# A chunked delta-rule recurrence on TensorE: products of a head pair on 64x128 and 128x128 stationaries, v and y turned on the whole array, and a new order of instructions

## The chip, the cores and the metric

The kernel runs on one core of a Trainium2 chip. The metric is the device time of one execution in microseconds, lower is better. Five engines work beside each other, each in its own program order: TensorE (PE, with its weight loads listed apart as PEld), VectorE (DVE), ScalarE (ACT), GpSimd (POOL) and SyncE (SP, which issues the DMAs here).

## The reference

Two layers over 256 positions of width 2048, batch 1. Layer 0 is an RWKV-7 time mix, a recurrence over time with a 64x64 state for each of 32 heads, then a squared-ReLU MLP. Layer 1 is forgetting attention over shared keys and values, then another MLP. The change lies in the recurrence and what surrounds it:

```python
def rwkv7_recurrence(r, decay, k, v, a, b):
    # S_t = S_{t-1} diag(decay_t) + (S_{t-1} a_t) b_t^T + v_t k_t^T ;  y_t = S_t r_t
    ...
y = rwkv7_recurrence(rh, dh, kh, vh, -kk, kk * ah)
mu = jnp.mean(y, axis=-1, keepdims=True)
var = jnp.mean(jnp.square(y - mu), axis=-1, keepdims=True)
y = ((y - mu) * lax.rsqrt(var + LNX_EPS)).reshape(B, S, D)
y = y * lnx_w + lnx_b
bonus = jnp.sum(rh * kh * r_k, axis=-1, keepdims=True) * vh
out = ((y + bonus.reshape(B, S, D)) * g) @ w_o
```

## The kernel before

Activations lie transposed: 128 channels on the partitions, 256 positions along the free axis, 16 such tiles (`xT`, and the operands `opA`, `opB`, each split into a high and a low part). A large product reads its weights in pieces of 512 KB (`load_split`): SP issues the load of `wr`, ACT casts it to the high part `wh`, DVE subtracts to the low part `wl`, and TensorE multiplies high by high, high by low and low by high, in fp32r, 12 products per step of 128 input rows (`mm3`, `gemm_steps`). The small products of the recurrence are plain fp32, and the profile lists each of these as two instructions.

The 32 heads are worked in eight units `u` of four heads. A tile of 128 partitions holds two heads, h = 0 on the lower 64 partitions (`HA`) and h = 1 on the upper (`HB`); q = 0, 1 are the two tiles of the unit. Time is cut into four chunks c of 64 positions. For each unit

- `prep` makes decays, keys and the scaled vectors and stores them to scratch in HBM;
- `inv` builds a 64x64 triangular inverse for each head and chunk, by fp16 products on 64x64 quarters of the array;
- `rec` (`rec_steps`) does the recurrence. It loads r, k, b, v and the inverse; forms the masked products of the keys and b with r (`g2a`, `g2b`) and with a diagonal of decays (`bta`, `btb`), 32 products 64x64x64 in each of two steps, on all four quarters of the array; the bonus sums (`bs`, 16 products with one column); then four chunks of three dependent steps. In the first, z from the state (`zp`, a 128x64 stationary); in the second, u = inverse times z (`up`, 64x64) and r times the state (`yp`, 64x64); in the third, the new state (`sp`) and y (`yp`), both on 128x64 stationaries from `L2`. Between the steps DVE and ACT copy the result out of the bank `zyus` (`zt`, `Tt`, `yt`). At the end come the group norm of y, 32 products 64x64 that turn y back (`yp`) and multiply v by the bonus (`vp`), the gain `lnw`, the bias `lnb`, the gate, and the split into `opA`.

The order of the work is written out by hand for each engine. Each generator is a stream (`gk`, `gr`, `gv` and `wo` are the large products, `la`, `lw`, `lg` and `gate` the low-rank ones, `mk`, `mr`, `mv` their inputs). `record` cuts each stream into pieces by step and engine; `ORDER_A` and `ORDER_B` list these pieces, as `rec3P` for the next TensorE piece of unit 3, and `replay` issues them in that order. Stage A covers projections and part of the inverses; stage B, the recurrence and the rest, with `gv` and `wo` pieces in between. After the replay the rest of the `wo` product (k = 12 to 15), the MLP and layer 1 follow, which the change leaves alone but for the order of the rows of `w_o`.

Of the kernel before, what the change touches and what calls it, by code (L numbers as in the profile page):

```python
# [94 lines left out]
STREAMS_A = (["first", "h", "mk"] + [f"gk{g}" for g in G4] + ["la", "lw", "lg", "gate"] + [f"prep{u}" for u in range(8)]  # L95
# [3 lines left out]
firstG firstP lwQ*2 gk0Q firstS gk0Q prep0Q*2 firstP firstV*2 firstS firstP firstG firstV firstP firstV firstP  # L99
firstS*2 hV*2 hG hV*2 hG lwV hV hG lwP lwV hV hG lwP gk0S lwV hG hV gk0S lwP lwV hG hV lwP lwV gk0S hG lwV lwP gk0S  # L100
mkV hG lwP gk0V mkS lwV*2 lwP mkV gk0V lwP gk0P mkV gk0Q hV gk0Q mkS gk0V hG mkV*2 gk0P lwV mkS gk0V mkV laQ mkV lwP
laV gk0P mkS hV gk0S mkV hG gk0S mkV gk0P gk0V mkS lwV gk0S mkV gk0S gk0V lwP gk0P mkV gk0Q gk0V mkS mkV*2 laP gk0V
gk0P mkS mkV gk0Q mkV laV mkS gk0P laV mkV hV gk0S mkV laP hG gk0S hV gk0P laV mkS hG gk0V mkV laP gk0S gk0V laP gk0S
lwV gk0P laQ lwV mkV gk0V mkS lwP mkV lwP gk0V gk0P mkV gk0Q laV mkS laV laP mkV hV laP mkV gk0P hG laV mkS laV mkV hV
laP lwV laP hG mkV gk0P gk0S gk0Q laV mkS gk0V gk0S mkV lwP gk0V laP lwV gk0P gk2Q mkV laV mkS hV lwP mkV hG hV laP
gk0S laV gk0P hG lwV gk0S mkV gk0V mkS lwP mkV laP gk2S gk0V gk0P gk2S lwV gr3Q mkV laV mkS lwP gk2V laP lwS mkV gr3Q
lwS gk2P mrV lwS laV mrS lwV laV mrV laP gk2V laP gr3S gk0P mrV gk2Q laV gr3S laV mrS gr3V laP gk0S mrV laP prep0S mrV
gk2P gr3Q prep0S gk0V prep0S gr3V prep0S gr3P lgV gr3Q laS prep0V mrS gr3S mrV gr3S mrV prep0P gr3V gk2S prep0P prep0V
mrS gk2S gr3P mrV prep0S mrV prep0S gr3V prep0S gr3P gk2V gk2Q prep0S gk2V mrS gr3S lgV gk2P gr3Q mrV gr3S gr3V mrV
gr3P gr3V gr3S mrS gr3V gr3Q gr3P mrV gr3S mrV gr3V mrS gk2P mrV gk2Q gk2S mrV gk2V mrS gr3P mrV gk2S mrV gk2V mrS  # L110
prep0P mrV gr3S gr3Q mrV gr3P gr3V mrS prep0S mrV prep0S mrV prep0S gk2P mrS prep0S mrV gr3S mrV gr3P gr3S gr3V mrS
gr3V prep0S gr3Q gr3P mrV gr3S mrV prep0S gr3V mrS gk2P gk2S prep0V gk2Q mrV gk2V gr3P gk2S mrV prep0V mrS mrV gr3P
gr3S gk2V mrV gk2Q gr3V mrS gk2P gr3S mrV prep0V mrV gr3P prep0S gr3V mrS prep0Q gr3S prep0V gk1Q mrV prep0S gr3P
prep0S prep0V gr3V gr3S lgV gr3V gr3P gk2S prep0V gk1Q gk2V prep0Q gk2P gk2S prep0V*2 gk2V prep0Q gr3P prep0V gk2S
gk1Q prep0V gk2V prep1S prep0Q gr3P prep1S prep0V gk2S prep0Q gk2V gk2P gr3S gr3V gk1S gr3Q prep1S gr3Q gk1V gk2P gk1Q
prep1S inv0Q gk1S prep1V gk2P gk1V gk1S gk1V gk1Q inv0Q prep1P gk1S prep1P inv0Q prep1V gk1V gk1P prep1S prep2Q prep1S
gk1Q prep1S gk1P prep1S gk1S gk1V gk1P gk1S gk1V gk2P gk1Q gk1S gk1V gk1P gk1S gk1V prep1P gk1Q gk1S gk1V gk1P prep1S
prep2Q prep1S*2 gk1P prep1S gk1S prep1S gk1V gk1P gk1S lgQ prep1S gk1V gk1P prep1V gk1S prep1V gk1V gk1P gk1S prep1V
gk2Q gk1V prep1S gk1P prep1V gk1S prep1Q prep1V*2 prep1S*2 gk1V gk1P prep1Q gk1S prep1V*2 gr0Q gk1V prep1Q gk1P gk1S
prep1V gk1V gk1P prep1V gk2S gr0Q prep1V prep1Q gk2V gk1P prep1Q gk2S gk2V gk1P lgQ gr0S gr0V gk1P gr0S gr0V lgP gr0Q  # L120
gk1S gk1V prep2S gk2P lgV prep2S*3 lgP gr0S prep2V gr0S gr0P gr0V*2 lgV prep2P gr0Q prep2P prep2V gr0S prep2P prep2S
gr0V prep2S lgP prep2S*2 gr0P lgV prep2S*3 lgP prep2S*2 gr0P lgV lgQ prep2S gr0S prep2V lgP gr0S prep2V gr0P prep2V*2
prep2S prep2V*2 prep2S*2 gk2P prep2Q prep2V*2 prep2Q gr0S prep2V prep2Q lgP prep2V*2 gr0P prep3S prep2Q prep3S gr0V
prep2Q gr0V gr0Q lgP gr0V gr0P lgV gk2Q lgV prep3S lgV prep3S gr0P prep3V prep3P*2 prep3V prep3P prep3S prep4Q prep3S
lgP prep3S prep4Q prep3S gr0P lgV gr0Q prep3S*3 lgP prep3S gr0S lgP lgV gr0S gr0V lgP gk2S gr0V gk2S gr0P gk2V lgQ
prep3S gk2V gr0S lgV prep3S gk2P gr0Q gr0V gr0S lgV gr0V gr0P prep3V gr0Q prep3V gr0P prep3V*2 prep3S prep3V*2 prep3S
lgP prep3S prep3Q prep3V*2 prep3Q gr0S gr0P gk3Q lgV gr0S prep3Q gr0V*2 lgP gr0S prep3V gk3Q gr0S gr0P gr0V*2 lgV lgP
gk3Q prep3V gr0P prep3V prep3Q mvV gk3S prep3Q lgP gk3V gk3S gk3V gk2P gk3Q gr0P gk3S gk2V gk2S gk3V prep5S lgP
prep5S*2 gr0P gr2Q prep5S lgS prep5V lgS gk3P gr0V lgS gr0S prep5P gk3S gr0Q prep5P mvS gr0Q prep5V gk3S mvV prep5P
gk3S gk3V prep5S gk3P gk3V prep5S gr2Q prep5S gk3V prep5S mvV gr2Q gk3P prep5S*3 gk3P prep5S*3 gk3P mvS prep5V gk3S  # L130
prep5V gk3S gk3P prep5V gr2S*2 mvV gk3V prep5S inv0P gk3V gr2S prep5Q inv0P prep5S gr2V prep5S gr2Q gk3P inv3Q inv0V
inv3Q inv0V inv0S inv3Q gr2V inv0Q gr2P gr2S inv0V gr2Q gr2V*2 gr2P gr2S mvV gk3Q gr2V mvS gk3P mvV gr2S mvV prep5V
mvS gr2V gr2P gr2S mvV gr2Q mvV gr2V mvS gr2P mvV gr2S mvV gr2V mvS inv3P mvV gr2Q mvV inv3P prep5V mvS prep5V inv0P
gr2S inv2Q gr2P inv3V inv2Q*2 inv3V inv3S prep5Q inv0V inv3Q gr2P gr2S inv3V inv0V*2 inv3P gk3S gr2V inv0P inv3V gr2P
inv3V*2 inv3P inv0V gk3S gr2P inv3V gr2V gk3V inv3P gr2Q gr2S inv0P gk3V inv3S gr2P gr2V gateQ inv3S mvV inv0S mvV
inv0S inv3P prep5V*2 gr2S inv2P inv3V inv2P mvS prep5Q gr2V inv0P inv1Q gk3P inv2V inv1Q*2 inv2V inv2S gk3Q inv0V
inv3P inv2Q gr2S mvV gr2P inv3S mvV inv3S gr2V mvS prep5V inv3P gr2S mvV inv0P inv3V inv0S gr2P gr2V inv0S mvV gk3Q
inv3P prep5V gr2S inv0P prep5V inv3S prep5Q gr2P inv3S inv0V prep5Q prep4S gr2V prep4S inv3P prep4S inv0P inv3V prep4S
gr2P inv0S prep4V inv0S gr2S inv3P inv0P gk3S gr2V prep4P inv3S inv0V gr2P gk3Q inv3S prep4V gk3V inv3P gk3S inv0P
inv3V inv0S prep4P gk3V inv0S inv3P prep4S gv0Q prep4S inv0P prep6Q inv3S inv0V gr2P inv3S prep4S inv3P prep4S gk3S  # L140
inv0P inv3V inv0S prep4P inv2V gk3V inv0S inv3P prep4S prep6Q inv2P prep4S inv3V inv0P prep4S inv2V gr2P inv3Q prep4S
inv2V prep4S inv2V prep4S inv0V gk3P gr2S prep4V gk3S gr2Q prep4V gateP gk3S prep4V mvS prep4V prep4S prep4V*2
prep4S*2 gk3P prep4Q prep4V*2 prep4Q gateS prep4V prep4Q gk3P gateQ prep4V gk3S prep4V prep4Q gr2V gk3P prep4Q gv0S
gk3V gr2Q gk3V gv0Q gk3P gv0S gk3V gv0V gv0Q gk3P gv0V mvV gv0Q mvV gk3P mvS mvV*2 mvS gateP gk3V gk3S prep6S mvV
prep6S mvV prep6S inv2P gateV gv0Q prep6S inv0P inv1P inv2V gv0S gateQ inv1P gv0S inv0V gv0P inv0Q mvS inv1V gv0S
inv4Q gv0V inv4Q inv1S gv0P gv0V inv4Q gv0S inv1V gateQ prep6V inv1Q gv0P gv0S gv0V*2 inv2P gv0S gv0V gr1Q gv0P inv2S
gv0V inv2S inv1V gv0Q mvV prep6P gv0S mvV gv0P prep6V mvS gv0V gv0P mvV gv0S mvV gv0V mvS gv0P mvV gr1Q mvV mvS inv4P
mvV inv4P inv2P inv4V inv5Q inv1P inv5Q gateP inv4V inv4S inv5Q inv2V inv4Q inv1V gr1S gateP inv1V gateS gr1V gr1S
gateQ inv1V gv0P gr1V gr1Q gateV gv0Q gateQ prep6P gv0S gv0V gv0P prep6S*3 gr1P prep6S gv0S gv0V gv0P gr1S gateQ gr1V
gr1P gr1S gr1V gv0P gr1Q gr1S gr1V gr1P gr1S gr1V gr1P gv0Q gv0S gv0V prep6P gv0S gv0V gv0P prep6S*2 gr1Q prep6S gr1P  # L150
prep6S gr1S prep6S gr1V gv0P gr1S prep6S gr1V gr1P gv0S prep6V gr1Q gv0V gr1P prep6V gv0S prep6V gv0V prep6S gv0P
prep6V gr1S gr1Q prep6V*2 prep6Q prep6S*2 gr1P gr1V gr1S prep6Q prep6V*2 gr1V gv0P prep6Q gr1S prep6V gr1Q gr1V gr1P
gr1S prep6V gr1V prep7S prep6Q gv0P prep7S prep6V gv1Q gr1S prep6Q gr1V gr1P gv0S gv0V prep7S gv0Q prep7S gv0Q gateP
gv0Q gr1S prep7V gv0Q*2 gr1V gr1S gv0Q prep7P gr1V gv0Q prep7P gv0Q prep7V gv1Q prep7P prep7S*2 gateP prep7S*4 gr1P
gv1Q prep7S gateV prep7S*2 inv2P inv1P prep7S inv1V gr1P gateS prep7V inv2S gateQ inv2S prep7V gateQ gr1P gr1S prep7V
# [99 lines left out]
def trunk_kernel(ctx: ExitStack, tc: tile.TileContext, xin, vecs, bfv, c32, c16, w_rkv, w1, w2, a1, a2, g1, g2,  # L255
# [360 lines left out]
    pp = ppctx.enter_context(tc.tile_pool(name="proj", bufs=1, reuse_waits="tile"))  # L616
    hT = pp.tile([P, KT, T + 1], F32, name="hT")
    dT = xT
    gh = pp.tile([P, 2, T], F32, name="gh")
    rs = gh[:, 0, :]  # L620

    def first_steps():
# [730 lines left out]
```

## Time and profile before

| | us |
|---|---|
| median of 3 runs (lowest, highest) | 2446.46 (2446.16, 2447.48) |
| the profiled execution's own time | 2446.65 |
| its span, first to last instruction | 2444.9 |
| PE busy in the span | 2407.0 |
| DVE, ACT, POOL busy | 1520.3, 1246.9, 217.0 |
| first and last product of `zyus` start | 343.9, 569.3 |

A busy time counts an instruction from its start to its modelled end; products overlap, so that the busy time of a group of products is not their price. The price of one is read from the distance between starts. A product's row gives the stationary as rows*columns and then the moving operand. An idle time is given with what ended it; "issue" there means that nothing the profile shows was waited for.

### The profile page before, as it was taken

Reading aid. Unit: us, or ns where it says so; the run is one execution under the profiler, and the core shown is the slowest. Engines: PE = TensorE matmul, PEld = TensorE weight load, DVE = VectorE, ACT = ScalarE, POOL = GpSimd, SP = SyncE. Lnnn points to the kernel's source line nnn. Section 1 sums busy time; section 2 is a strip of 40 time slices with the busy share of each in tenths; the row PEclk is TensorE's granted clock in tenths of the full one; section 3 lists DMA queues with packets and bytes.
Section 4 is the critical chain, followed back from the end, with each engine's and each line's share of the span. In section 5 each row is a group of like instructions: output and inputs, shape, how many; then the busy total and the mean of one; then the engine's idle time right before and its main releaser. Section 6 shows DMA issues by size and latency. Waiting matters only on the chain.

```text
span 2444.9 us, 45691 instructions
## 1 busy us (share of the span) xinstructions
PE 2407.0 (98%) x18336; PEld 2077.2 (85%) x18336; DVE 1520.3 (62%) x2210; ACT 1246.9 (51%) x1983; POOL 217.0 (9%) x218
## 2 busy tenths in 40 slices
PE   8999999999999999999999999999999999999998
PEld 6999877789888888888888888888888888888886
DVE  8878767766754555555567555877654555555554
ACT  3767655545544543443545545555554543443543
POOL 2000012221200000000101000101100000000101
PEclk9999999999999999999999999999999999999999
DMA  5766786656656656666655566545656666666653
GB/s 166 238 230 233 258 262 192 185 184 204 206 190 192 192 187 195 190 189 197 187 185 172 179 193 192 169 150 186 201 184 196 189 190 192 192 187 196 189 188 122
DMA packets 276564, 472.55 MB, mean 193 GB/s; under 512 B 23280, under 2 KB 70656, under 8 KB 276352
## 3 DMA queue, kind: packets, MB, share of 16 engines
q1 hardware_dynamic: 276352, 469.64, 61.3%
q8 instruction: 143, 2.34, 0.4%
q14 instruction: 69, 0.57, 0.1%
HBM read 445.44 MB, written 24.13 MB: 192 GB/s over the span
## 4 chain that ended last, share of the span: by engine, by line
PE 92%; DVE 4%; issue 2%; DMA 1%; ACT 0%; POOL 0%; SPq 0%; POOLq 0%; DVEq 0%; ACTq 0%
PE mmw L245 32%; PE mmd L245 28%; PE mm L251 9%; PE mmn L245 7%; PE mmv L251 4%; PE mmv L245 4%; PE zyus L251 2%; PE i L251 1%; DVE wl L251 1%; PE lps L251 1%; PE mm L245 1%; DVE xs L251 1%; PE lo L251 1%; PE mmg L251 1%; DVE wl L245 0%
## 5 line engine op out<-in xcount | busy, mean ns | idle before, releaser
L245 DVE TENSOR_TENSOR wl<-wr,wh 128x1024 fp32r<-128x1024 f32 (+1 forms) x784 | 810.0, 1044 | 698.4 <-ACT wh L245 623.1
L245 ACT CAST wh<-wr 128x1024 fp32r<-128x1024 f32 (+1 forms) x784 | 702.6, 901 | 833.2 <-PE mmd L245 344.3
L245 PE MATMUL mmw<-opB,wh 128*128 128x512 f32 x1280 | 321.2, 393 | 0.2 <-ACT wh L245 0.2
L245 PE MATMUL mmd<-wh,opA 128*128 128x512 f32 x1024 | 315.8, 390 | 0.0
L245 PE MATMUL mmd<-wh,opB 128*128 128x512 f32 x1024 | 315.8, 390 | 0.0
L245 PEld LDWEIGHTS mmw<-opB,wh 128*128 128x128 f32 x1280 | 230.3, 189 | 42.2 <-ACT wh L245 0.4
L245 PE MATMUL mmw<-opA,wh 128*128 128x512 f32 x1024 | 256.7, 392 | 0.0
L245 PEld LDWEIGHTS mmd<-wh,opA 128*128 128x128 f32 x1024 | 191.7, 188 | 39.5
L245 PEld LDWEIGHTS mmd<-wh,opB 128*128 128x128 f32 x1024 | 191.7, 188 | 39.5
L245 PEld LDWEIGHTS mmw<-opA,wh 128*128 128x128 f32 x1024 | 184.4, 189 | 33.3 <-ACT nln L245 0.3
L251 ACT CAST wh<-wr 128x512 fp32r<-128x512 f32 x240 | 144.9, 617 | 116.4 <-PE mm L251 50.1
L245 PE MATMUL mmd<-wl,opA 128*128 128x512 f32 x512 | 199.3, 389 | 0.0
L245 PE MATMUL mmd<-wl,opB 128*128 128x512 f32 x512 | 199.2, 389 | 0.0
L251 DVE TENSOR_TENSOR wl<-wr,wh 128x512 fp32r<-128x512 f32 x240 | 169.3, 719 | 38.3 <-ACT wh L251 32.1
L245 PEld LDWEIGHTS mmw<-opB,wl 128*128 128x128 f32 x1280 | 174.5, 190 | 13.5 <-DVE wl L245 1.0
L245 POOL TENSOR_TENSOR ms<-mt 128x512 f32<-128x512 f32 x64 | 78.5, 1239 | 1158.8 <-ACT mt L245 1158.8
L245 PE MATMUL mmw<-opB,wl 128*128 128x256 f32 x1280 | 178.6, 282 | 0.6 <-DVE wl L245 0.6
L251 PE MATMUL mm<-opA,wh 128*128 128x256 f32 x896 | 171.4, 291 | 0.2 <-DVE opA L251 0.2
L245 PEld LDWEIGHTS mmw<-opA,wl 128*128 128x128 f32 x1024 | 139.7, 190 | 10.0
L251 PEld LDWEIGHTS mm<-opA,wh 128*128 128x128 f32 x896 | 141.7, 192 | 3.8 <-DVE opA L251 0.4
L245 PE MATMUL mmw<-opA,wl 128*128 128x256 f32 x1024 | 142.8, 282 | 0.0
L251 PE MATMUL mm<-opA,wl 128*128 128x256 f32 x448 | 127.2, 284 | 0.0
(273 smaller groups left out, 3338.0 us busy)
## 6 DMA issues: line engine op xcount, KB each, us to landing
wr<-in_mlp_w_up_dram SPq DMA_DIRECT2D x256, 512.0 KB, 4.1
wr<-in_mlp_w_down_dram SPq DMA_DIRECT2D x256, 512.0 KB, 3.7
wr<-in_w_rkv_dram SPq DMA_DIRECT2D x96, 512.0 KB, 4.7
wr<-in_w_kvf_dram SPq DMA_DIRECT2D x64, 512.0 KB, 3.7
wr<-in_w_o_dram SPq DMA_DIRECT2D x32, 512.0 KB, 4.6
wr<-in_fox_w_q_dram SPq DMA_DIRECT2D x32, 512.0 KB, 3.4
wr<-in_fox_w_o_dram SPq DMA_DIRECT2D x32, 512.0 KB, 4.4
wr<-in_g_dram SPq DMA_DIRECT2D x8, 512.0 KB, 4.3
```

Of the source, the lines that this page charges most:

```text
L245: return f(*a, **k)
L251: return op[2](*op[3], **op[4])
```

## The change

- The products of k and b with r and with the decays use `BK`, which holds for each head its 64 columns of b and of k side by side: one 64x128 stationary times 128 columns (r and the diagonal, side by side in `RD`). 16 products a unit in two steps take the place of 64. `BK` is loaded in four pieces of 128 KB with runs of 256 bytes, in place of two loads of 256 KB.
- The bonus sums become four products a unit with `r_k` broadcast over 64 columns and 256 moving columns, whose result stands on all 64 partitions of a head; ACT copies it to `vb`, and DVE multiplies `vb` by v. For that v is loaded once more (`Vt`) and turned by four 128x128 transposes (`vT`).
- In a chunk, r times the state moves into the first step, ahead of `zp`. The new state and y come from one 128x128 stationary of `L2` (64 columns each), four products a chunk, in the last chunk too. ACT copies y out in two pieces where DVE did it in one.
- y is turned by four 128x128 transposes (`yT`); the bonus `vb` is added from SBUF.
- As the rows of a unit now stand by head, w_o is loaded with its rows reordered, in two DMAs for each piece (`by_pair`), the gate `gt` in two, and gain and bias are reordered once by four small products (`ln_steps`).
- `inv` no longer breaks its first 32 products into two pieces.
- `ORDER_A` and `ORDER_B` are written anew throughout. They list 573 TensorE pieces before and 575 after, 376 and 440 of SP, 831 and 817 of DVE, 669 and 765 of ACT, 82 and 82 of POOL. At the start of stage A, the products `gk2` and `gk0` now come ahead of `lw` and `la`.

```diff
+    def by_pair(w, k0, col):
+        def load(raw):
+            for q in range(2):
+                dma(raw[q * CH:(q + 1) * CH], w[(k0 + q) * P:(k0 + q + 1) * P, col:col + 512]
+                    .rearrange("(h v) n -> v h n", h=2))
+        return load
...
+    def ln_steps():
...
+                mm(ps[H[q]], C("ident")[H[h], H[h]], cols[H[h], q], start=True, stop=True, skip_group_check=True)
+            V.tensor_copy(lnp.rearrange("p w (u h) -> p h w u", h=2)[:, h], ps)
...
-            if c == 3:
-                yield
...
-        b8, k8 = c8(ld("b", s_b)), c8(ld("k", s_k))
+        BK = rp.tile([P, 8, 2, CH], F32, tag="BK", name="BK", bufs=1)
+        for h in range(2):
+            for x, src in ((h, s_b), (1 - h, s_k)):
+                ldma(BK[H[h], :, x, :], src[u, H[h]].rearrange("p (c t) -> p c t", t=CH))
...
+        Vt = rp.tile([P, NCH, P], F32, tag="Vt", name="Vt", bufs=1)
...
-        ga, gb = pairs(R8, "g2a", "g2b")
-        V.tensor_tensor(L8[:, :, 64:128], ga, bcast(C("mle"), 8), op=ALU.mult)
-        V.tensor_tensor(L8[:, :, 128:192], gb, bcast(C("mle"), 8), op=ALU.mult)
-        yield
-        ga, gb = pairs(dg, "bta", "btb")
-        cp("bt", L8[:, :, 0:64], ga)
-        cp("kt", L8[:, :, 192:256], gb)
-        yield
+        for q in range(2):
+            banks = [side(f"g2{h}").rearrange("p (x c t) -> p x c t", x=2, c=NCH) for h in range(2)]
+            for c in range(NCH):
+                n = slice((NCH * q + c) * CH, (NCH * q + c + 1) * CH)
+                for h in range(2):
+                    mm(banks[h][:, :, c, :], BK[H[h], NCH * q + c].rearrange("p x t -> p (x t)"), RD[H[h], :, n], ...)
+            for h in range(2):
+                d, m = slice(h * CH, (h + 1) * CH), slice((1 - h) * CH, (2 - h) * CH)
+                V.tensor_tensor(L2[:, q, :, h, m], banks[h][:, 0], bcast(C("mle"), NCH), op=ALU.mult)
+                cp("bt", L2[:, q, :, h, d], banks[h][:, 1])
+            yield
...
-        for c in range(8):
-            for h in range(2):
-                quad(bp[H[1 - h], c:c + 1], c8(k2)[H[h], c, :], vcol("rk", p0 + c // NCH)[H[h], :])
-        db = rp.tile([P, 8, CH], F32, tag="db", name="db", bufs=2)
-        V.tensor_tensor(db, bcast(C("ids"), 8), bp[:, :, None].to_broadcast([P, 8, CH]), op=ALU.mult)
+        for q in range(2):
+            for h in range(2):
+                mm(bp[h][H[q]], vcol("rk", p0 + q)[H[h]].to_broadcast([CH, CH]), k2[H[h], q, :], ...)
+        vb = rp.tile([P, 2, T], F32, tag="vb", name="vb", bufs=2)
+        for h in range(2):
+            S.copy(vb[:, h, :], bp[h])
+        yield
+        V.tensor_tensor(vb, turned("vT", lambda c: Vt[:, c, :]), vb, op=ALU.mult)
+        yield
...
         for c in range(NCH):
...
-            halves(zp, lambda q, h: RA[:, h, q, c, :], True)
+            for q in range(2):
+                for h in range(2):
+                    mm(bank[H[1 - h], 2 + h, q, :], R8[H[h], 4 * q + c, :], Tt[H[h], h, c, q, :], start=q == 0, ...)
+            for q in range(2):
+                for h in range(2):
+                    mm(zp[H[h], q, :], RA[:, h, q, c, :], Tt[:, h, c, q, :], start=False, ...)
...
-            if c < NCH - 1:
-                halves(sp, lambda q, h: L2[:, q, c, 192 * h:192 * h + CH], False)
-            halves(yp, lambda q, h: L2[:, q, c, 64 + 64 * h:128 + 64 * h], False)
...
-            cp("yt", yt[:, :, c, :], yp)
+            for q in range(2):
+                for h in range(2):
+                    mm(bank[:, 2 + h, q, :], L2[:, q, c, h, :], Tt[:, h, c, q, :], start=False, ...)
...
+            for h in range(2):
+                S.copy(yt[H[1 - h], c], bank[H[1 - h], 2 + h])
...
-                quad(yp[H[h], c, :], y3[H[h], c, :], i)
-                quad(vp[H[h], c, :], Tt[H[1 - h], h, c % NCH, c // NCH, :], db[H[1 - h], c, :])
+        yp = turned("yT", lambda c: yt[:, c].rearrange("p q v -> p (q v)"))
```

More of the change, by code (lines that the diff above doesn't have):

```diff
@@ L327, in load_split @@
         raw = wraw.tile([p, nk, n], F32, tag="wr", name="wr")
-        dma(raw, src)
+        if callable(src):
+            src(raw)
+        else:
+            dma(raw, src)
         hl = []
```

336 lines of the change are left out of this document (173 added, 163 removed).

## The prediction

> **What bounds the kernel now.** I read the page first, then stretches of the span, then who waited, then single instructions.
>
> ```profile
> PE 2407.0 (98%) x18336; PEld 2077.2 (85%) x18336; DVE 1520.3 (62%) x2210; ACT 1246.9 (51%) x1983; POOL 217.0 (9%) x218
> PE 92%; DVE 4%; issue 2%; DMA 1%; ACT 0%; POOL 0%; SPq 0%; POOLq 0%; DVEq 0%; ACTq 0%
> ```
>
> TensorE is 92% of the chain that ended last. The table of stretches (length, then busy time and instructions of PE, PEld, DVE, ACT, POOL, then granted clock, DMA share, GB/s) says where it isn't full:
>
> ```profile
> 0.00:100.00 100.00, 91.72 (x606) 80.17 (x607) 89.01 (x181) 53.05 (x107) 14.46 (x25) 0.95 0.58 186
> 100.00:300.00 200.00, 199.00 (x2284) 185.56 (x2283) 151.44 (x277) 137.39 (x263) 0.40 (x2) 1.00 0.73 243
> 300.00:580.00 280.00, 264.84 (x5771) 224.61 (x5770) 202.12 (x373) 141.04 (x298) 52.65 (x62) 0.98 0.66 201
> 580.00:2444.90 1864.90, 1851.43 (x9681) 1586.80 (x9679) 1077.69 (x1382) 915.38 (x1318) 149.54 (x129) 1.00 0.60 187
> ```
>
> The change lies in the third row. There DVE is busy 72%, ACT 50%, the DMA engines 66%; TensorE is idle 280 - 264.84 = 15.2 us. Who waited in that stretch (engine, line, releaser: total us, times, longest):
>
> ```profile
> PE i L251 <- issue: 3.4, 2, 2.9
> PE g2a L251 <- issue: 1.8, 1, 1.8
> PE bs L251 <- issue: 1.7, 2, 1.1
> PE btb L251 <- issue: 1.5, 2, 1.2
> PE vp L251 <- issue: 0.7, 1, 0.7
> PE bta L251 <- issue: 0.5, 1, 0.5
> ```
>
> 9.6 us of the 15.2 wait for no data ("issue"), 6.2 of them inside the dense bursts of 64x64 products that the change takes out. So TensorE's work sets this stage, and the question is what the new products cost on TensorE itself.
>
> **The change part by part.** The old prices first. In the order of time (start, length):
>
> ```profile
> 444.13 0.22 PE L251 MATMUL g2b<-xT,b 64*64 64x64 f32 x1
> 444.13 0.22 PE L251 MATMUL g2a<-xT,k 64*64 64x64 f32 x1
> 444.14 0.22 PE L251 MATMUL g2b<-xT,k 64*64 64x64 f32 x1
> 444.15 0.22 PE L251 MATMUL g2a<-xT,b 64*64 64x64 f32 x1
> 444.19 0.22 PE L251 MATMUL g2b<-xT,b 64*64 64x64 f32 x1
> ...
> 446.50 0.27 PE L251 MATMUL g2a<-xT,k 64*64 64x64 f32 x1 [1.81 <-issue]
> 347.29 0.69 PE L251 MATMUL zyus<-Tt,L 128*64 128x64 f32 x16
> 1262.48 1.04 PE L245 MATMUL ytp<-k,y 128*128 128x128 f32 x8
> 135.12 1.03 PE L251 MATMUL lo<-th,w 96*128 96x256 f32 x4
> ```
>
> Four products on the four quarters start together, and the next four 58 ns later (444.13 to 444.19): 14.5 ns an instruction. Sixteen on 128x64 last 0.69 us, less one's 0.22: 0.47/15 = 31 ns. A transpose of 128 columns: (1.04 - 0.27)/7 = 0.11 us. An instruction with 256 moving columns: (1.03 - 0.38)/3 = 0.217 us. The counts of before:
>
> ```profile
> L251 PE MATMUL g2a<-xT,b 64*64 64x64 f32 x128 | 9.7, 222 | 0.0
> L251 PE MATMUL bs<-vec,k 64*64 64x1 f32 x256 | 9.3, 195 | 2.2 <-issue 1.7 <-DVE L L251 0.5
> L251 PE MATMUL yp<-k,yt 64*64 64x64 f32 x256 | 10.5, 233 | 0.9 <-DVE yt L251 0.8
> L251 PE MATMUL zyus<-Tt,L 128*64 128x64 f32 x448 | 20.1, 230 | 1.8 <-ACT Tt L251 1.7
> ```
>
> There are eight groups of 128 like the first (`g2`, `bt`), and `vp` has 256 like `yp`.
>
> The weight loads decide what the new products cost. Durations (min/median/max) of a 64-column and a 128-column load, and two rows in time:
>
> ```profile
> L251 PEld LDWEIGHTS bs<-vec,k x256: 129/135/223, 336.0 to 540.5; 64*64 64x64 f32 x128
> L245 PEld LDWEIGHTS sp<-kT,qT x64: 187/192/218, 1536.7 to 1641.0; 128*128 128x128 f32 x64
> 336.02 0.60 PEld L251 LDWEIGHTS bs<-vec,k 64*64 64x64 f32 x18 [0.36 <-issue]
> 569.41 0.30 PEld L251 LDWEIGHTS mm<-opA,wh 128*128 128x128 f32 x2
> ```
>
> `bs` multiplies by one column, so nothing but the loads can space it: 18 loads in 0.60 us, (0.60 - 0.135)/17 = 27 ns, that is 55 ns on each of the two quarters it alternates between. Two 128-column loads that wait for no product start 0.30 - 0.19 = 0.11 us apart. A full stationary thus takes 0.11 us to load, however few columns move.
>
> *State and y in one 128x128 product.* Before 448 x 0.031 = 13.9 us. After, 8 units x 4 chunks x 4 products x 2 = 256 instructions with 64 moving columns. They move in the 58 ns of the quarters, but their loads come every 0.11 us: 28.2 us. Ends: 256 x 0.058 = 14.8 us if the load hid, 28.2 if it doesn't. I take the second, since the rows show the load alone: +14.3 us. r times the state, `zp` and `up` keep their 768 instructions.
>
> *Products on 64x128.* Before 1024 x 14.5 ns = 14.8 us. After, 256 instructions of 128 moving columns (0.11 us, by the transposes' row). No row shows two halves of 64 rows at once; the quarters do overlap, so I take two at a time: 128 x 0.11 = 14.1 us, -0.7; the other end, one after another, is 28.2, +13.4.
>
> *Bonus and turns.* `bs`: 256 x 27 ns = 7.0 us goes; 64 instructions of 256 columns, four quarters at once, come: 16 x 0.217 = 3.5. `yp` and `vp`: 512 x 14.5 ns = 7.4 go; 64 transposes x 0.11 = 7.0 come. Together -3.9 us (0 if the bonus overlaps two at a time). `lnp`'s four products and two copies fall into the start, where TensorE waits anyway; without that cover they are below 1 us.
>
> *Changes of the array's shape.* Going into and out of 64-row or 64-column products costs extra:
>
> ```profile
> 331.44 0.40 PE L251 MATMUL mmv<-wl,opB 128*128 128x512 f32 x1
> ...
> 331.77 0.27 PE L251 MATMUL g2a<-xT,b 64*64 64x64 f32 x1
> ...
> 334.27 0.22 PE L251 MATMUL btb<-xT,k 64*64 64x64 f32 x1
> 334.42 0.74 PE L251 MATMUL mmv<-wh,opB 128*128 128x512 f32 x2
> 335.00 0.40 PE L251 MATMUL mmv<-wl,opB 128*128 128x512 f32 x1
> ```
>
> The large product ends at 331.84, the first quarter product at 332.04: 0.20 us, where 0.01 is usual. Back: from 334.49 two large products need until 335.16, 0.67 us, and the third 0.24: 0.67 - 0.48 = 0.19 more. I followed the TensorE pieces through both orders and counted changes of shape: 43 before and 76 after in stage A (the inverses lie more thinly there), 192 and 194 in B. 35 x 0.19 = +6.7 us. Transposes and the 128x128 products need none; r times the state, now ahead of `zp`, adds one inside its step, and both are in the count.
>
> *Waits.* No burst of `rec` is longer than 32 instructions afterwards (64 to 128 before), so I let its 6.2 us of "issue" go, and half of the 3.4 of `i`, whose pieces now always have at least one other piece between them: -7.9 us. Ends 0 and -9.6. What is late next is the chain of the chunk: its third step grows from 16 x 0.031 = 0.50 to 8 x 0.11 = 0.88 us; one large piece stands behind most steps and covers a copy:
>
> ```profile
> 59.26 1.43 PE mm L251 x12
> ```
>
> [...]
>
> *Other engines and queues.* DVE loses 32 copies `yt` and the full-width `db`; ACT gets 64 half copies and `vb`; both have a quarter or more to spare in the third row. SP issues 64 more DMAs and `BK` moves in runs of 256 bytes: the DMA engines are 66% busy, and loads are listed several pieces ahead. I cost these at nothing; if a load came late, `wh` and then TensorE would wait, up to 5 us in all by the 5.6 us of data waits in the stage now. `gk2` and `gk0` ahead of `lw` at the start: zero, between -5 and +5, since
>
> ```profile
> PE lps L251 <- DVE xs L251: 4.8, 3, 4.2
> ```
>
> is what `lw` waits for now, and the new first product has one cast and two more DVE steps ahead of it.
>
> Sum: +14.3 - 0.7 - 3.9 + 6.7 - 7.9 = +8.5 us on the profiled execution's 2446.65 us (span 2444.9; the median, 2446.46, is 0.2 lower): 2455.
>
> **The rivals.**
> - *The new order takes the waits.* The work grows by 16.4 us, but all 15.2 us of idle time in the stage and the 4.8 at the start go: -3.6, 2443. For it: pieces of one inverse stand further apart. [...]
> - *The full stationary loads behind the product* (the other side): 0.058 in place of 0.11 us, 13.4 us less, -4.9: 2441.6. Below 0.077 us a product the change stops costing. Against it are both rows of loads.
> - *The chain or the halves.* If the chunk's chain sets the time, 32 x 0.38 = 12 us come on top: 2467. If the 64-row halves don't overlap, 13.4 + 3.5: 2472. Against the first: `wo` and `gv` pieces stand between the steps.
> - *"Issue" stays*: 2463.
>
> **How the numbers follow.** Forecast 0.42, order 0.20, hidden load 0.12, chain or halves 0.16, issue 0.10. The range, 2437 to 2470, cuts about 0.1 at each end; the forecast's own is 2448 to 2462. A measurement can tell about 0.2%, 4.9 us. Faster by more: 0.07 from the forecast's lower tail, 0.11 from the order, 0.09 from the hidden load: 0.27. Same: 0.10 + 0.07 + 0.03 = 0.20. Slower: the rest, 0.53.
>
> **What would show it.** Right: products `zyus` with a 128x128 stationary start 0.11 us apart; pairs of 64x128 start together, 0.11 apart; fewer PE waits on "issue" between 300 and 580 us; the first `mmw` some 8 us later. Wrong: the 128x128 products 0.06 apart, the halves one after another, or TensorE idle well below 7 us or above 20 in the stage.

## The result, and the profile after

The changed kernel takes 2464.11 us (median of 4 runs, 2460.03 to 2467.07) against 2446.97 us for the kernel before on the same chip: ratio 1.0067, 95% interval 1.0054 to 1.0081. The profiled execution took 2461.68 us with a span of 2459.9, 15.0 us more than the one before. The number lay near the forecast. The reasons hold only in part, as the rows show.

The page of the changed kernel, first the busy row of TensorE, then the chain of waits by engine:

```profile
PE 2418.2 (98%) x16744; PEld 2088.9 (85%) x16744; DVE 1516.4 (62%) x2196; ACT 1268.3 (52%) x2079; POOL 220.1 (9%) x218
PE 89%; DVE 4%; issue 2%; DMA 2%; ACT 2%; SPq 0%; POOL 0%; POOLq 0%; DVEq 0%; ACTq 0%
```

Its stretches, in the columns of the table shown in the prediction:

```profile
0.00:100.00 100.00, 88.50 (x615) 81.86 (x616) 81.73 (x166) 46.73 (x92) 16.21 (x25) 0.97 0.53 175
100.00:300.00 200.00, 199.11 (x2571) 181.30 (x2569) 160.05 (x297) 144.42 (x282) 0.00 (x0) 1.00 0.77 251
300.00:580.00 280.00, 274.49 (x3874) 235.52 (x3865) 192.39 (x344) 159.01 (x379) 57.10 (x64) 0.99 0.81 209
580.00:2460.00 1880.00, 1856.10 (x9703) 1590.22 (x9701) 1082.27 (x1391) 918.19 (x1328) 146.76 (x129) 0.99 0.59 185
```

In the recurrence stage TensorE is idle 280 - 274.49 = 5.5 us, where it was 15.2. At the start it is idle 11.5 us instead of 8.3. The fourth row hides the main thing: 1880 - 1856.10 = 23.9 us idle there, against 13.5 before. Most of these 10.4 us (8.8, by the rows below) sit behind the recurrence, in the rest of the `wo` product (k = 12 to 15, four groups, 192 products), which is the same work in both kernels; a wait of 2.4 us stands just ahead of it. I call this rest the tail: from its first product to the first `mmw` of the MLP. Its first and last products, and the stretch, before:

```profile
L245 PE MATMUL mm<-opA,wh x128: 278/283/287, 592.9 to 616.5; 128*128 128x256 f32 x128
592.90:616.70 23.80, 23.51 (x193) 23.10 (x193) 20.44 (x27) 15.85 (x30) 9.76 (x7) 1.00 0.63 202
```

And after:

```profile
L254 PE MATMUL mm<-opA,wh x128: 279/283/581, 596.5 to 632.5; 128*128 128x256 f32 x128
596.50:632.70 36.20, 27.10 (x192) 26.11 (x193) 27.65 (x36) 17.21 (x34) 12.51 (x9) 0.81 0.64 182
```

So the first `mmw` comes 16.0 us later (632.7 against 616.7), and 12.4 of these arise in the tail: 36.2 us instead of 23.8 for the same products, with 9.1 us idle (0.3 before) and a granted clock of 0.81. The products themselves are busy for 27.10 us instead of 23.51: behind the first long wait in the tail the granted clock is 0.50, from 616.6 to 629.2 us, and there they start 0.21 us apart, where 0.12 is usual. So, if that clock is a result of the waits, which no run isolates, they cost some 3.6 us more than their own length. Everything ahead of it, start and recurrence together, costs 3.6 us. From here on "stage" means the time up to the first product of the tail.

Who waited from the last turn of y (592) to the first `mmw` in the changed kernel (PE, then SP's own queue):

```profile
PE mm L254 <- DVE wl L254: 6.2, 2, 3.5
PE mm L254 <- ACT wh L254: 5.2, 2, 2.9
SPq L254 <- DVE wl L254: 15.1, 3, 8.5
SPq L254 <- DVE xT L254: 11.4, 3, 5.2
```

One of PE's four waits lies just ahead of the tail and counts to the 3.6 us. It is the end of the recurrence's own chain, y of unit 7 to `opA`, with the cast of `wh` behind it on ACT:

```profile
595.28 0.62 ACT L260 CAST opA<-y 128x512 fp32r<-128x512 f32 x1 [1.54 <-DVE y L260]
595.80 3.24 ACT L254 CAST wh<-wr 128x512 fp32r<-128x512 f32 x6
596.47 0.74 PE L254 MATMUL mm<-opA,wh 128*128 128x256 f32 x4 [2.36 <-ACT wh L254]
```

Large products between the last turn of y and the first `mmw`, before (first fence) and after:

```profile
575.60:616.69 41.09, 40.80 (x336) 40.39 (x337) 30.37 (x42) 24.18 (x44) 9.75 (x7) 1.00 0.74 243
```

```profile
592.70:632.69 39.99, 28.53 (x204) 27.33 (x204) 29.60 (x38) 19.46 (x38) 12.51 (x9) 0.83 0.61 173
```

Less the tail's 192, 144 products stood behind that turn and covered its chain; now it is 12. The other three waits, 9.0 us, are waits for casts of weights (`wl`, `wh`, `wl`). SP in the changed kernel, in order of time:

```profile
597.85 2.27 SPq L254 DMA_DIRECT2D wr<-in_w_o_dram  x3
603.27 0.38 SPq L254 DMA_DIRECT2D xr<-in_x_dram  x1
603.69 0.60 SPq L254 DMA_DIRECT2D wr<-in_w_o_dram  x1
...
609.11 0.38 SPq L254 DMA_DIRECT2D xr<-in_x_dram  x1
609.59 2.60 SPq L254 DMA_DIRECT2D wr<-in_w_o_dram  x4
```

And before:

```profile
589.99 9.01 SPq L245 DMA_DIRECT2D wr<-in_w_o_dram  x4
599.23 0.97 SPq L245 DMA_DIRECT2D xr<-in_x_dram  x2
603.87 0.37 SPq L245 DMA_DIRECT2D wr<-in_mlp_w_up_dram  x1
```

Before, the last pieces of w_o stood ahead of the fourth load of `xr`. After, they stand behind it. `xr` has three buffers, so that load waits until DVE has added an earlier one into `xT`, and the weights wait with it (SP's 11.4 us on `xT` above). The casts have moved too (DVE, ACT and PE, changed kernel):

```profile
610.20 5.75 DVE L254 SCALAR_TENSOR_TENSOR opB<-xT,vec,opB 128x256 fp32r<-128x256 f32 x4
615.88 0.68 DVE L254 TENSOR_TENSOR wl<-wr,wh 128x512 fp32r<-128x512 f32 x1
616.61 0.58 PE L254 MATMUL mm<-opA,wl 128*128 128x256 f32 x1 [3.48 <-DVE wl L254]
...
621.32 2.16 ACT L254 CAST wh<-wr 128x512 fp32r<-128x512 f32 x4
621.98 1.22 PE L254 MATMUL mm<-opA,wh 128*128 128x256 f32 x4 [2.86 <-ACT wh L254]
```

DVE makes four parts of the next operand before it makes the `wl` that TensorE waits for, and again before the `wl` of the third wait. ACT casts the last weights at 621.32, behind operand work that waits for `xT`, though the last of their transfers had landed at 617.31. So the loads do come later than before, but each of the three waits ends with a cast that stood behind other work on its engine, not with a transfer. Nothing in the diff orders this part: `replay` ends with the recurrence, and behind it the compiler's planner places the instructions of each engine. What the diff changes there is `by_pair`: each piece of w_o now takes two DMAs.

### The profile page after: what moved, and what is told of

Read it like the earlier page. It is cut to its first block, busy times and chain, and to the rows that moved or that the text cites. A ratio compares the mean times of both kernels' runs of the same rounds, so it can differ in the third digit from the quotient of the medians.

```text
span 2459.9 us, 42671 instructions
## 1 busy us (share of the span) xinstructions
PE 2418.2 (98%) x16744; PEld 2088.9 (85%) x16744; DVE 1516.4 (62%) x2196; ACT 1268.3 (52%) x2079; POOL 220.1 (9%) x218
## 4 chain that ended last, share of the span: by engine, by line
PE 89%; DVE 4%; issue 2%; DMA 2%; ACT 2%; SPq 0%; POOL 0%; POOLq 0%; DVEq 0%; ACTq 0%
PE mmw L254 33%; PE mmd L254 28%; PE mm L260 7%; PE mmn L254 7%; PE mmv L254 4%; PE mmv L260 3%; PE zyus L260 2%; PE i L260 1%; DVE wl L260 1%; PE g L260 1%; DMA wr<-in_w_o_dram 1%; PE mm L254 1%; PE lo L260 1%; DMA wr<-in_w_rkv_dram 1%; PE lps L260 0%
```

## The experiments

For each kernel: the ratio to the kernel before, the first product of the tail, and the tail's length, from the same rows as above.

| run | ratio (95%) | tail starts | tail, us |
|---|---|---|---|
| before | 1 | 592.9 | 23.8 |
| changed kernel | 1.0067 (1.0054 to 1.0081) | 596.5 | 36.2 |
| third_cols | 1.0043 (1.0029 to 1.0056) | 589.2 | 36.5 |
| before_pairs | 0.9971 (0.9961 to 0.9981) | 586.8 | 25.6 |
| a_as_before_16 | 1.0157 (1.0143 to 1.0171) | 618.2 | 36.4 |
| g2_quarters | 1.0082 (1.0068 to 1.0096) | 597.3 | 38.8 |
| before_mix | 1.0076 (1.0063 to 1.0089) | 594.5 | 37.5 |
| after_old_order | 1.0125 (1.0109 to 1.0140) | 607.9 | 38.1 |
| probe_quarter | 1.0180 (1.0166 to 1.0193) | 624.6 | 36.5 |
| probe_full | 1.0143 (1.0129 to 1.0157) | 613.5 | 38.0 |
| before_two | 1.0047 (1.0033 to 1.0061) | 597.5 | 33.8 |
| after_xr | 1.0059 (1.0044 to 1.0074) | 602.5 | 30.6 |
| third_cols_xr | 1.0017 (1.0007 to 1.0028) | 589.6 | 29.7 |
| before_third | 1.0045 (1.0031 to 1.0059) | 604.1 | 23.8 |

Every kernel that loads w_o in halves has a tail of 30 to 39 us; the three that don't have 24 to 26.

**The third step undone (third_cols).**

```diff
-                    mm(bank[:, 2 + h, q, :], L2[:, q, c, h, :], Tt[:, h, c, q, :], ...)
+                    for o in ((0, 1) if c < NCH - 1 else (1 - h,)):
+                        mm(bank[H[o], 2 + h, q, :], L2[:, q, c, h, o * CH:(o + 1) * CH], Tt[:, h, c, q, :], ...)
```

> The changed kernel, with the third step of a chunk taken back from 128x128 stationaries to column halves of 64 (448 instructions instead of 256; in the last chunk the y half alone). Same pieces, same order, same results. Theory: the 128x128 products are held up by their weight loads, 0.109 us for each instruction; column halves run side by side at 0.028 us, as they did in the kernel before. Then the third step goes from 27.8 us to 448 x 0.028 = 12.5 us (-15.3). The price: the steps are no longer full-array products, so 43 more changes of shape (313 instead of 270) at 0.19 us give back 8.2 us. Net -7 us: about 2457 against the changed kernel's 2464 (ratio to before 1.004). Rival one, the loads hide and 0.109 us comes from something else that stays (the copies between the steps): no gain in the step and +8 us, 2472. Rival two, a shape change into 64-column products costs nothing: the whole 15 us come back, 2449.

Measured 2455.59 us: by the ratios 0.0024 or 5.9 us below the changed kernel, in the stage 7.3 us (589.2 against 596.5), close to the 7 expected and far from both rivals. In the changed kernel the 128x128 products do come at the pace of their loads, and the 64x128 pairs side by side (order of time, changed kernel):

```profile
470.34 1.00 PE L260 MATMUL zyus<-Tt,L 128*128 128x64 f32 x8
...
416.52 1.16 PE L260 MATMUL g<-xT,BK 64*128 64x128 f32 x16
```

The first is (1.00 - 0.22)/7 = 0.111 us from start to start, the second (1.16 - 0.27)/15 = 0.06: two at a time.

**The pairs alone (before_pairs).**

```diff
+                    mm(banks[h][:, :, c, :], BK[H[h], NCH * q + c].rearrange("p x t -> p (x t)"), RD[H[h], :, n], ...)
```

in place of `pairs()` of the kernel before, with `BK` and `RD` of the change; the order as before, with the few extra loads and copies beside their old ones.

> The kernel before, with one part of the change alone: the products of k and b with r and with the decays on 64x128 stationaries with 128 moving columns (16 products a unit instead of 64, in the loads with runs of 256 bytes), all else and the order of TensorE as before, the order lists of the other engines altered only where this part has other loads and copies. Theory: the two 64-row halves run side by side, so that the products cost 0.7 us less, and the waits on 'issue' inside the dense bursts of 64 instructions (3.8 us at g2a, bta and btb in the kernel before) are gone: about -4 us, 2442.5 (ratio 0.998). Rival one: the halves run one after another, +13 us, 2460. Rival two: the waits have another cause and move to the next product, -1 us. Rival three: the short runs of the loads delay the large products' weights, +2 to +5 us.

Measured 2439.23 us, 7.0 us (0.29%) under the kernel before, and the stage 6.1 us shorter. This is the fastest kernel of the study, ahead of both. It gained more than the 4 expected, though part of "issue" only moved: its waits on it, in the recurrence stage,

```profile
PE i L258 <- issue: 4.1, 2, 2.8
PE zyus L258 <- issue: 3.0, 2, 1.6
```

are 7.1 us, against 9.6 before and none of them in the products of k and b. So the second rival holds in part, and the 2.5 us of waits with the 0.7 expected of the products leave some 3 of the 6.1 us without a known cause.

**Stage A in its old order (a_as_before_16).** Only the two lists differ from the changed kernel, from their first line on:

```diff
-firstG firstP gk2Q gk0Q gk2Q firstS gk0Q prep0Q*2 firstP ...
+firstG firstP lwQ lwQ gk0Q firstS gk0Q prep0Q prep0Q firstP ...
```

`ORDER_A` takes the sequence of the kernel before, and the pieces of `inv1` and `inv4` that do not fit follow at the head of `ORDER_B`.

> The changed kernel with the pieces of stage A in the order of the kernel before; the inverse pieces that the new order had spread into A (units 1 and 4) come at the start of stage B instead, between gv pieces. Same instructions in all. Changes of the array's shape 249 instead of 270. Theory: the start (+3.2 us of TensorE idle in the first 100 us, and products at half clock until 25 us) is the price of gk2 and gk0 ahead of lw and la, and goes; 21 changes of shape at 0.19 us are 4 us less; against that stand new waits on the chain of the inverses at the start of B, 1 to 4 us. Net -4 us: 2460 (ratio 1.005), with 8 to 9 us of TensorE idle in the first 100 us in place of 11.5. Rival one: the start costs the same in both orders because the first data decide it (idle stays at 11.5), and only the shape changes show: -1 to +2 us. Rival two: the clustered inverses wait on their own chain for more than the changes save: +5 us or more.

Measured 2483.8 us, 19.7 us above the changed kernel (22 by the ratios): rival two. Its first 100 us and a stretch early in B:

```profile
0.00:100.00 100.00, 91.50 (x608) 80.20 (x609) 89.13 (x182) 53.17 (x107) 14.45 (x25) 0.97 0.59 187
340.00:380.00 40.00, 28.61 (x673) 23.12 (x673) 17.13 (x32) 15.93 (x36) 6.20 (x8) 0.76 0.67 196
```

The start is back at 8.5 us idle, so 3.0 us of the changed kernel's 11.5 are the price of `gk2` and `gk0` ahead of `lw`. But the packed inverses leave TensorE idle 11.4 us of 40 in B, at a clock of 0.76. The seam was my own, so the run says nothing on how good the new order is; it shows what spreading the inverses avoids.

**The pairs undone (g2_quarters).**

```diff
-                    mm(banks[h][:, :, c, :], BK[H[h], NCH * q + c].rearrange("p x t -> p (x t)"), RD[H[h], :, n], ...)
+                for x in range(2):
+                    for h in range(2):
+                        for o in range(2):
+                            mm(banks[h][H[o], x, c, :], BK[H[h], NCH * q + c, o, :], RD[H[h], x, n], ...)
```

> The changed kernel with the products of k and b taken back to 64x64 quarters (64 products a unit, 1024 instructions instead of 256, in dense bursts of 64 instructions), nothing else altered. It is to show what the waits on 'issue' are. Theory of instruction supply: bursts in which the array takes an instruction every 15 ns run dry, so that PE waits on 'issue' reappear in these products, 2 to 5 us in the recurrence stage, where the changed kernel has 0.9; the work itself +0.6 us; 13 changes of shape less, -2.5 us. Net 0 to +3 us: 2464 to 2467. Rival: the waits of the kernel before belonged to its order (a late operand that the profile doesn't show) and don't come back with the small products: 'issue' stays below 1 us, time 2462.

Measured 2466.09 us, stage +0.8. PE's waits on "issue" in the recurrence stage, this run first; the changed kernel has one row of 0.9.

```profile
PE g L260 <- issue: 2.7, 3, 1.1
PE bs L260 <- issue: 1.0, 1, 1.0
PE i L260 <- issue: 1.0, 1, 1.0
```

They come back (4.7 us) in the products that were made small again and right behind them, as the theory had it for these dense bursts of short instructions. That the bursts don't fix the sum alone is seen in before_third below.

**Three parts in the old order (before_mix), and all parts in the old order (after_old_order).** The first is the changed kernel's source with the chunk loop of the kernel before and `yT` read accordingly; the second has the changed kernel's loop. Between them stands

```diff
-            if c < NCH - 1:
-                halves(sp, lambda q, h: L2[:, q, c, h, h * CH:(h + 1) * CH], False)
-            halves(yp, lambda q, h: L2[:, q, c, h, (1 - h) * CH:(2 - h) * CH], False)
+            for q in range(2):
+                for h in range(2):
+                    mm(bank[:, 2 + h, q, :], L2[:, q, c, h, :], Tt[:, h, c, q, :], ...)
```

and r times the state, moved as in the change. In both the lists are those of before, each added piece next to the one it replaces (`vT` right behind `bs`, the loads of `Vt` behind that of `Yf`).

> The kernel before and its order, with three parts of the change: the products of k and b on 64x128, the bonus by broadcast products, v and y turned by 128x128 transposes (with the layout by head that these need: w_o in two DMAs a piece, gate in two, gain and bias reordered). Not changed: the first step, r times the state in the second step, state and y as column halves in the third, and the order (the few added instructions stand next to those that they replace). Theory: these parts gain, and the loss of the whole change lies in the 128x128 third step and in the new order. From the run with the pairs alone (7.0 us under the kernel before): bonus 10.1 to 4.1 us (-6.0), turns 12.0 to 8.9 us (-3.1), 4 more changes of shape (+0.8): 8.3 us less, 2431 (ratio to before 0.994). Rival one: the waits on 'issue' of the bonus products move on to the next small products, as some did in the run with the pairs: 2435. Rival two: the added DMAs (v once more, w_o in two pieces) make weights late: 2441 or more.

> The changed kernel, all of its parts, but in the order of the kernel before (the few added instructions stand next to those that they replace, and the inverse has its first products in two pieces again). Against the run named before_mix it has the 128x128 third step and r times the state in the first step; against the changed kernel it differs by the order alone. Theory: the third step costs 9.4 us in work (256 x 0.109 against 448 x 0.028 with entries, 29.4 against 20.0 us) and three changes of shape, 0.6; so 2431 + 10 = 2441, and the rest of the changed kernel's 17 us over the kernel before, about 23 us against this run, is the order: 18 more changes of shape (3.4 us), 3.2 us at the start, and the rest inside stage B. Rival one: the order is worth nothing, the work is the loss: 2460 to 2464. Rival two: with the longer third step this old order stalls on the chain of the chunk: more than 2450, with PE waits on zt and Tt well above 3 us.

Measured 2467.8 and 2478.33 us, 37 us above what I expected of each. The waits of PE in before_mix from 300 us on begin with

```profile
PE vT L270 <- DMA Vt<-v: 6.5, 3, 3.5
PE mm L264 <- DVE wl L264: 6.3, 2, 3.2
```

The first is my placing of the loads. The second is the tail, 13.7 us longer than before with the order of the kernel before in front of it. That sent me to the tail of every run, and to the last four experiments. The two runs differ by 10.5 us, near the 10 expected for the third step, but both are disturbed, so that this confirms nothing.

**What a change of shape costs (probe_quarter, probe_full).** One more product in 120 steps of `gk` and `gr`:

```diff
+                if probe and k > ks[0]:
+                    mm(ps[0][HA, 0, 0:8], zero[HA, 0:CH], ones[HA, 0:8], ...)
```

and in the control `mm(ps[0][:, 0, 0:8], zero, ones[:, 0:8], ...)`.

> The price of a change of shape by itself. The changed kernel with one more product in 120 steps of the large products gk and gr: a 64x64 stationary of zeros times 8 columns, added into the same sum, so that results stay; each takes the array from whole products to a quarter and back. Theory (0.17 to 0.20 us each way, as in the recurrence): 120 x (0.37 + about 0.03 for the two instructions) = +48 us, 2512. Rival: the change costs only where the next operand is late anyway, and is hidden behind the weight loads of a full stream: +6 us or less.

> The control for the run before: the same 120 added products with a 128x128 stationary of zeros, 8 columns, no change of shape. Theory of load-bound stationaries: two instructions at 0.109 us, 120 x 0.22 = +26 us, 2490. Rival: the load of a product with few columns hides behind the large products around it (which take 0.12 to 0.24 us each): +2 to +6 us.

Measured 2492.28 and 2483.53 us, less than expected of both. The stage grows by 28.1 and 17.0 us (48 and 26 expected), 0.23 and 0.14 us for each product. Part of it fills idle time: in the first 100 us TensorE is busy 92.52 and 92.83 us instead of 88.50. With these 4.0 and 4.3 us added it is 0.27 and 0.18. So a full stationary with 8 columns costs two instructions of about 0.09 us, near the load's 0.11: here it didn't hide. A detour to a quarter and back costs at most 0.27 us, product included, 0.13 a change where I had 0.19.

**Two DMAs for a piece of w_o in the kernel before (before_two).** The tail's eight pieces alone; recurrence, layout and both lists untouched.

```diff
+            for q in range(2):
+                dma(raw[q * CH:(q + 1) * CH], w[k0 * P:(k0 + 2) * P, col:col + 512]
+                    .rearrange("(k p) n -> p k n", p=P)[q * CH:(q + 1) * CH])
...
-            gemm_group(w_o, 512 * g, opAH, opAL, o_evac_for(g), range(12, 16), po[g] if g < 2 else None)
+            gemm_group(w_o, 512 * g, opAH, opAL, o_evac_for(g), range(12, 16), po[g] if g < 2 else None, halves=True)
```

> The kernel before, with one edit outside the recurrence: the eight pieces of w_o that follow the written-out order (k = 12 to 15) are each loaded by two DMAs of 64 partitions and 256 KB instead of one of 512 KB, same rows, same place. Theory: most of the loss of the changed kernel lies here. From the last turn of y to the first mmw it has 40.3 us for 204 large products (24.4 us at 0.1195 us), 15.9 us lost; the kernel before has 41.4 us for 336 products (40.2 us), 1.2 us lost; the four other kernels with w_o in halves lose 14.7 to 18.4 us, the one with the pairs alone 3.0. After the written-out order the compiler's planner orders SP, and with two DMAs a piece it puts loads of xr, which wait for a buffer that DVE's addition into xT gives back, ahead of loads of w_o. So this kernel should lose 11 to 13 us: 2458 (ratio 1.005), with PE waits on wl and wh in the last 52 us before mmw. Rival one: the loss comes from the end of the new order (a single piece of w_o behind the last turn), then nothing changes here: 2446. Rival two: half-size DMAs are slower as such: waits on wr all along, no SP wait on xT.

Measured 2458.54 us, 11.3 us (0.47%) slower, as expected. Tail 33.8 us instead of 23.8; the stage varied by 4.6. In the tail:

```profile
PE mmw L245 <- ACT wh L245: 3.8, 1, 3.8
PE mm L245 <- DVE wl L245: 3.4, 1, 3.4
...
SPq L245 <- DVE xT L245: 9.4, 3, 4.7
```

SP's wait on `xT` (0.5 us in the kernel before) appears with nothing changed but the split. The casts stand in another order here too: where ACT makes four `wh` in a row at 608.34 in the kernel before, it makes two at 615.35 and two at 619.04, with operand work between them. Here one cast does wait for its transfer as well: ACT stands 2.9 us before the two at 615.35, and PE 1.1 us behind them.

**`xr` and `part` loaded by POOL (after_xr, third_cols_xr).**

```diff
-            ldma(xr, xsrc[:, 2 * kp:2 * kp + 2, :])
+            G.dma_start(xr, xsrc[:, 2 * kp:2 * kp + 2, :])
...
-                ldma(fl(part), s_p[kp])
+                G.dma_start(fl(part), s_p[kp])
```

> The changed kernel, with the loads of xr and part after the written-out order issued by POOL in place of SP; nothing else. Theory: SP then goes from one piece of w_o to the next without waiting for an addition into xT, and the three waits of 3.3 to 4.1 us behind it go; the wait of 2.8 us for opA right after the last turn of y stays. 2464 - 11 = 2453 (ratio 1.003). With that the recurrence itself would come out at about the time before, and the sum of its terms (+8.5 forecast) would be near +1. Rival: the halves of w_o arrive late for reasons of their own (transfer time, buffers), the waits on wl and wh stay: 2462 to 2465.

> The changed kernel with both edits: the third step in column halves (8.5 us less in its own run), and xr and part loaded by POOL (11 us less expected). If the two losses are independent: 2455.6 - 11 = 2444.6 (ratio 0.9993), level with the kernel before; if one hides the other: 2450 or more.

Measured 2461.74 and 2450.87 us: 2.0 and 6.4 us less than without the edit, by the ratios, where I had 11; the intervals of the first pair overlap, those of the second do not. The tail is 5.6 and 6.8 us shorter in the two profiles. SP's wait on `xT` falls from 11.4 to 1.1 us, but one long wait of PE stays (after_xr):

```profile
PE mm L254 <- DVE wl L254: 4.4, 1, 4.4
SPq L254 <- DVE wl L254: 31.1, 7, 10.2
SPq L254 <- DVE xT L254: 1.1, 1, 1.1
...
619.35 4.39 DVE L254 SCALAR_TENSOR_TENSOR opB<-xT,vec,opB 128x256 fp32r<-128x256 f32 x4
```

DVE again makes four parts of the operand ahead of the weights. So taking these loads from SP gives back about half of the tail's loss. It doesn't follow that SP's queue was that half: the planner moved casts with it (between the operand work of the second and the third group ACT makes five `wh`, where the changed kernel has one). What is left hangs, by this row, on DVE's order. No run changed the order of one engine alone. The stage of after_xr came out 6.0 us longer in its profile, that of third_cols_xr 0.4; the first shows 2.0 us of waits for `Vt` and a clock of 0.98, and why is open.

**The third step alone (before_third).** The kernel before with the changed third step, r times the state in the first step, and y copied by ACT.

```diff
-                halves(sp, lambda q, h: L2[:, q, c, 192 * h:192 * h + CH], False)
-            halves(yp, lambda q, h: L2[:, q, c, 64 + 64 * h:128 + 64 * h], False)
+            for q in range(2):
+                for h in range(2):
+                    mm(bank[:, 2 + h, q, :], L2[:, q, c, 128 * h:128 * h + 128], Tt[:, h, c, q, :], ...)
...
-                quad(yp[H[h], c, :], y3[H[h], c, :], i)
+                quad(yp[H[h], c, :], y3[H[1 - h], c, :], i)
```

> The kernel before, with one part of the change alone: state and y from one 128x128 stationary in the third step (four products a chunk, in the last chunk too), r times the state ahead of z in the first step, y copied out in two pieces by ACT where DVE did it in one; order as before. Changes of shape 229 instead of 235. Theory of load-bound products: the third step goes from 20.0 to 29.4 us (+9.4), changes of shape -1.1 us: about +8, 2454.5 (ratio 1.003). Rival one: with the old order the longer third step and the later copy of y stall the chain of the chunk: +12 us or more, with PE waits on Tt and yt above 5 us. Rival two: the step hides in waits that were there: within 3 us.

Measured 2457.87 us, 0.45% or 11 us slower; stage +11.2, tail unchanged. That is more than the 8 expected, and not by the chain: PE waits 1.9 us on `Tt` and 1.2 on `yt`. My edit had a second effect. Its last turn of y, start of the first group and of the last:

```profile
584.74 0.32 PE L265 MATMUL yp<-k,yt 64*64 64x64 f32 x3
...
586.49 0.33 PE L265 MATMUL vp<-db,Tt 64*64 64x64 f32 x4
```

1.75 us, where the kernel before needs 0.94 (574.38 to 575.32): y lies on the other half of the partitions, so that `yp` and `vp` now share two quarters. Eight times 0.8 is some 6.5 us of the 11.2. Against it, waits on "issue" fell from 9.6 to 3.1 us without an edit to the bursts. The third step's own price, by subtraction, is near 11 us; it was not isolated better than that. (Added up in the trace from each start to the next, without idle time, the `zyus` products rise by 17.8 us and the turn by 5.8, while all other products fall by 6.0 and idle time by 6.4.)

## Why the prediction was right, and where it was wrong

The forecast of 2455 lay 9 us from the median, inside its range. That it came so near is partly luck: the part ahead of the tail came out 4.9 us lower than the sum of the terms, and the tail, which had no term, 12.4 us higher. Of the signs set down beforehand, those on the new products and on "issue" came true; the first `mmw` came 16.0 us later instead of some 8, and 5.5 us of idle time in the stage from 300 to 580 us lie below the 7 that were to count against the forecast.

- **"Other engines and queues. ... I cost these at nothing ... up to 5 us in all."** This step failed. The 12.4 us of the tail are three quarters of the loss, and before_two shows 10.0 of them in a kernel that shares only the two DMAs. I counted the added DMAs and looked at how full the DMA engines are (66% then; 81% now, with TensorE idle for 5.5 us). I didn't ask who orders the instructions behind the written-out lists, nor what is queued behind a load that waits, or behind operand work on the engines that cast the weights. The row of the kernel before for the stage after 580 us looked harmless (13.5 us idle in 1865), and I took "left alone" at its word.
- **The third step, +14.3.** Right in kind and about in size: 0.111 us apart as forecast (0.11), not hidden. third_cols gives 7.3 us back after paying for its added changes of shape; before_third, corrected, about 11.
- **The pairs, -0.7.** The halves overlap (0.06 us), as taken; with the waits that go it was -6.1 in the stage of before_pairs, against -0.7 and 3.8 of waits.
- **Bonus and turns, -3.9.** No run isolates them; before_mix was spoilt by the loads of `Vt`. From start to start these products fell from 17.9 to 11.8 us, -6.1.
- **Changes of shape, +6.7.** Oversized: at the probe's 0.13 us and less, 35 are 4.6 us or less. Nor do the traces leave much room for them: added up from each TensorE start to the next, without idle time, all work ahead of the tail grew by 7.6 us (569.4 to 577.0), where the terms had 16.4. `zyus` gave +15.4, the products of k and b +0.5, bonus and turns -6.1, and all other products, in which most changes of shape would show, -2.2. (The granted clock was 0.50 from 15.7 to 25.9 us in the kernel before and from 18.2 to 25.0 in the changed kernel; that is in the last figure.)
- **Waits, -7.9.** "Issue" fell from 9.6 to 0.9 us: -8.7. The assumption on bursts was right in kind, and g2_quarters brings the waits back (4.7 us); but before_pairs keeps 7.1 us without the bursts of k and b, and before_third has 3.1 us with them. The waits on data and on other engines ahead of the tail rose by 5.2 us (12.4 to 17.7), so that all idle time there fell by 4.0 only. As to what the waits on "issue" are: each of the nine in the kernel before ended 1.3 to 1.6 us behind a transfer of instructions (last section).
- **The start, zero between -5 and +5.** +3.2 us, 3.0 of which the old sequence takes back (a_as_before_16).
- **The chain of y at the end of B** was in no term: 2.4 us, since 132 large products less stand behind the last turn.

The stage came to +3.6 us where the terms said +8.5. Start and last chain take 5.6 of that, so the rest ahead of the tail is about 2 us faster than before, not 8.5 slower. Of the rivals, "the new order takes the waits" (-3.6) came nearest to that in its number, not in its reason: work grew by 7.6 us instead of 16.4, and 4.0 us of idle time went instead of 20. The tail covered it. "The halves" and "the full stationary loads behind the product" are refuted by the rows of their products, "the chain" by PE's waits on `zt` and `Tt`, 1.7 us from 300 to 580 us, and "'issue' stays" by its 0.9 us.

## What to carry to other kernels

An edit to a load, even one that moves the same bytes, can reorder the queues of a region that nobody wrote out: compare the order of each queue and engine there, and look for a load that waits for a buffer ahead of weights, and for a cast of weights behind other work. Price the parts of a compound change one at a time: here the pairs alone are worth 0.29%, the full-array third step loses it, and the split of a load loses it again. Here a 128x128 stationary for 64 columns took 0.11 us, the pace of its loads, and two 64-column halves side by side 0.06 (two of 0.031 us in the kernel before).

## What the runs showed of the hardware

Beside POOL, DVE was slower than I had thought. In the kernel before, two parts of `opB` took 0.87 us, 0.48 each, while POOL was idle:

```profile
600.31 0.87 DVE L245 SCALAR_TENSOR_TENSOR opB<-xT,vec,opB 128x256 fp32r<-128x256 f32 x2
```

In the changed kernel four took 5.75 us, 1.48 to 1.52 each, while POOL added without a break:

```profile
609.89 1.54 POOL L254 TENSOR_TENSOR nacc<-nacc,nsq 128x512 f32<-128x512 f32 x1 [3.29 <-DMA part<-s_p]
611.39 1.48 POOL L254 TENSOR_TENSOR xr<-xr,part 128x512 f32<-128x512 f32 x1
612.83 1.44 POOL L254 TENSOR_TENSOR nacc<-nacc,nsq 128x512 f32<-128x512 f32 x1
614.24 1.44 POOL L254 TENSOR_TENSOR xr<-xr,part 128x512 f32<-128x512 f32 x1
```

Each of the four ended 0.28 us behind the end of one of these additions (the first at 611.71, behind 611.43), so that they went at the pace of POOL's instructions. A loss of about 4 us in four instructions (5.75 less two times 0.87), just ahead of the cast that TensorE waited for, is part of the tail's price (the kernel before took 3.74 us for four parts at 606.77, with POOL adding for part of that time).

The traces make me take the waits on "issue" for waits for instructions. The page lists a queue of instruction transfers, q8: 143 packets of 16 KB in the kernel before and 131 in the changed kernel, which is 64 bytes for each of TensorE's 36672 and 33488 products and loads. From 300 to 580 us, each of the 9 such waits of the kernel before ended 1.28 to 1.57 us behind the end of a q8 packet, and the two of the changed kernel 1.32 and 1.54 us behind one, though these packets come some 6 us apart in the kernel before (45 in those 280 us) and 9 in the changed kernel (31). My estimate from these counts alone is that a packet holds 256 instructions, as many as the 64 old products of k and b of one unit make with their loads.

These waits are not a fixed sum: the same recurrence had 9.6 us of them in the profile of the kernel before and 11.2 in that of before_two. Differences of a few us in the stage between two profiles should be read with that in mind.
